# Three edits to the change-over between chunks: which queue stores the output projection's sums, where the last residual tile lies, and where the halo of h lies

## The chip, the cores and the metric

The kernel runs on one core of a Trainium2 chip. The metric is the device time of one execution in microseconds (us), as the median of several runs. Five engines work side by side, each through its own instructions in order: TensorE (PE; its weight loads are listed as PEld), VectorE (DVE), ScalarE (ACT), GpSimd (POOL) and SyncE (SP). SP does no arithmetic here; its queue issues most of the DMA transfers, and POOL's queue issues others between its arithmetic. An instruction that waits for a semaphore holds up everything behind it on its own engine's queue.

## The reference, cut to what matters

Two sequences go through a two-layer trunk: a prompt of 2048 rows and a sample of 512 rows, each row 1024 wide, in float32. Layer 0 is windowed attention, layer 1 a Fourier mixer, and a norm follows. The change lies wholly in layer 0:

```python
def attention_layer(x, g, w_in, w_out, sink, rel_bias):
    h = rmsnorm(x, g)
    z = h @ w_in                       # q (16 heads of 64), k, v (4 heads of 64), gate (1024)
    ...
    o = banded_gqa_with_sink(q, k, v, rel_bias, sink)   # |i-j| <= 128, blocks of 128
    return x + (o * silu(gate)) @ w_out
```

The last line is where the change sits: `x` there is the residual, the product with `w_out` is the output projection, and their sum is the input of layer 1.

## The kernel before, in words

**Chunks.** Layer 0 is done in five chunks of 512 rows, in the order of the list `CHUNKS`: chunk 0 is the sample, chunks 1 to 4 are the prompt. For the window, a chunk that has rows after it in its sequence (chunks 1, 2 and 3) also needs the keys and values of the next 128 rows, its halo. The change calls chunks 1, 2 and 3 the inner ones.

**Every matmul is three.** Operands are split into a high and a low float32r part (`matmul3`, L86 to L88), so each tile of h, q, of the probabilities, of u and of the weights is a pair.

**One chunk.** `make_h` (L171 to L183) loads eight tiles `xk` of the transposed input (512 rows and, with a halo, 128 more), POOL multiplies each by the inverse norms (L173), ACT and DVE make the two parts of `h` (L176, L177) and, where there is a halo, the two parts of `hl` (L182, L183). The `xk` tiles have four places (tag `x`), so the fifth load waits until the first `xk` has been read for both h and hl. `kv_proj` projects k (tiles `kp`, and `kh` for the halo) and v (`vp`); ACT and DVE evacuate k to `kwin` (L253, L254), `kh` (L275) and v (L300, L301). `qg_proj` makes q (`qab`, two places, L334 to L337) and the gate for one pair of heads at a time; eight pairs `p` follow one another. For each, scores (L388), exponentials (L400, L404), transposes of the probabilities into `pts` (tag `pt`, two places, L420 to L422), the product with v (`av`, L434), and the gated result in `uT` (tag `uT`, eight places, one for each pair, L442 to L452).

**The change-over.** `out_proj` multiplies the eight `uT` with `w_out`, in two halves of 512 columns. A half has eight steps `mm(half, k)`, which fill four PSUM banks `op`, and then `evac(half)` (L473 to L485): for each of four row tiles, the residual is loaded into an `xr` tile (L483), DVE adds the bank to it (L484) and the sum is stored to `x1d` (L485). `xr` has three places, so the fourth residual of a half waits for the store of the first. Chunks 0 to 3 issue these loads and stores on SP's queue. The last chunk issues them on POOL's, and there a list `res_tile` of two further tiles serves the fourth residual of each half. The first part of half 0 runs within the last pair's attention; the rest (the list `tail`) runs after the next chunk's `make_h` has been called, and before the next chunk's `kv_proj`. For the change-over from chunk 0 to 1 the tail is called before `make_h`.

**PSUM.** One pool of six banks (tag `bank`) serves `op`, `kp`, `kh`, `vp`, `pt`, `av` and the projections of q and the gate in turn. After half 1, `kp` takes two banks, `kh` one and `vp` up to four, so `vp` needs banks of half 1 whose sums have been made and the bank of `kh`.

**Weights.** From chunk 1 on, `load_w` (L94) loads each split weight tile of 1 MB in one DMA on SP's queue into one of four places (tag `w`). At the change-over these are `wo` for half 1, then `wk` and `wv`, two each, then `wq` and `wg`. `wk` holds four of the eight steps of the k projection in each tile.

**Order.** A planner orders the instructions of each engine beforehand, from the order in which the code calls them, from its own estimate of durations and from the places that come free. So what is called early may still be placed late on a queue, and what stands ahead on a queue can have been called later. `after(ins, anchor)` only tells the planner to place one instruction after another; it adds no wait.

**Layer 1** reads `x1d` from HBM after chunk 4; its first tiles are those of chunk 0.

Of the kernel before, what the change touches and what calls it, by code (L numbers as in the profile page):

```python
# [8 lines left out]
F32 = mybir.dt.float32  # L9
F32R = mybir.dt.float32r  # L10
# [3 lines left out]
ALU = mybir.AluOpType  # L14
# [4 lines left out]
P = 128  # L19
# [12 lines left out]
LINE = 512  # L32
# [3 lines left out]
CHUNKS = [(2048, SEQ, T), (0, 0, SEQ), (512, 0, SEQ), (1024, 0, SEQ), (1536, 0, SEQ)]  # L36


def f32(ap):
    return ap.bitcast(F32)  # L40
# [3 lines left out]
def encoder(  # L44
# [3 lines left out]
    PE, ACT, DVE, POOL, SP = nc.tensor, nc.scalar, nc.vector, nc.gpsimd, nc.sync  # L48
# [4 lines left out]
    wp = wstack.enter_context(tc.tile_pool(name="wp", bufs=1, side="right"))  # L53
# [12 lines left out]
    x1d = dram.tile([T, D], F32, name="x1d")  # L66
# [8 lines left out]
    def bank(name):  # L75
        return psum.tile([P, 512], F32, tag="bank", name=name)
# [7 lines left out]
    def matmul3(out, a, b, start, stop, more=False):  # L84

        PE.matmul(out, a[0], b[0], start=start, stop=False, skip_group_check=more)  # L86
        PE.matmul(out, a[0], b[1], start=False, stop=False, skip_group_check=more)  # L87
        PE.matmul(out, a[1], b[0], start=False, stop=stop, skip_group_check=more)  # L88

    def load_w(c, n, name, lo_engine=None, late=None):  # L90

        w = wp.tile([P, 2, D], F32R, align_bytes=LINE, tag="w", bufs=4, name=f"w{name}")
        if c:
            SP.dma_start(f32(w), f32(wsd[n]))  # L94
            return w[:, 0], w[:, 1]
        w32 = stage[late is not None or n > 19 or n in (6, 7, 18, 19)](f"w32{name}")
        load = SP.dma_start(w32, w_in[n] if n < 20 else w_out[(n - 20) // 4, (n - 20) % 4])
        if late:
            after(load, late)
        ACT.copy(w[:, 0], w32)  # L100
        if lo_engine is None:

            for i in range(4):
                cs = slice(i * 256, i * 256 + 256)
                POOL.tensor_tensor(w[:, 1, cs], w32[:, cs], f32(w[:, 0, cs]), ALU.subtract)
        else:
            lo_engine.tensor_tensor(w[:, 1], w32, f32(w[:, 0]), ALU.subtract)
        if late or n not in LATE:
            (SP if lo_engine else POOL).dma_start(f32(wsd[n]), f32(w))
        return w[:, 0], w[:, 1]  # L110

    stage, res_tile = [], []

    def after(ins, anchor):

        if anchor is not None:
            tc.add_manual_dep(ins.ins, anchor.ins.name, ISSUE, reason="issue order")

    def attention_phase():

        with ExitStack() as es:
            ap = es.enter_context(tc.tile_pool(name="attn", bufs=1))
# [19 lines left out]
            def spread(c, inv):  # L142

                tok, lo_t, hi_t = CHUNKS[c]
                nt = min(640, hi_t - tok) // P
                invb = ap.tile([P, 640], F32, tag="invb", name=f"invb{c}")
                for i0 in range(0, nt, 4):
                    m = min(4, nt - i0)
                    ps = bank(f"ib{c}_{i0}")
                    dg = ap.tile([P, 4, P], F32, tag="tmp", bufs=2, name=f"dg{c}_{i0}")  # L150
                    DVE.tensor_tensor(
                        dg[:, :m], ident.unsqueeze(1).to_broadcast([P, m, P]),
                        inv[:, i0 : i0 + m].unsqueeze(2).to_broadcast([P, m, P]), ALU.mult,
                    )
                    PE.matmul(ps[:, : m * P], ones, dg[:, :m].rearrange("p i q -> p (i q)"), start=True, stop=True)
                    ACT.copy(invb[:, i0 * P : (i0 + m) * P], ps[:, : m * P])
                return invb

            def make_h(c, invb):

                tok, lo_t, hi_t = CHUNKS[c]
                n = min(640, hi_t - tok)
                hs, halo = [], []
                for k in range(KD):
                    if invb is None:
                        if k % 2 == 0:
                            xk2 = wp.tile([P, 2, CH], F32, align_bytes=LINE, tag="uT", bufs=8, name=f"xk{c}_{k}")
                        xk = xk2[:, k % 2]
                    else:
                        xk = ap.tile([P, D], F32, tag="x", bufs=4, name=f"xk{c}_{k}")[:, :640]  # L170
                    SP.dma_start(xk[:, :n], xT[k * P : (k + 1) * P, tok : tok + n])  # L171
                    if invb is not None:
                        after(POOL.tensor_tensor(xk[:, :n], xk[:, :n], invb[:, :n], ALU.mult), last_evac[0])  # L173
                    h = main.tile([P, 2, CH], F32R, align_bytes=LINE, tag="hT", bufs=8, name=f"h{c}_{k}")
                    gk = g0s[:, k : k + 1]
                    ACT.activation(h[:, 0, :], xk[:, :CH], AF.Copy, scale=gk)  # L176
                    DVE.scalar_tensor_tensor(h[:, 1, :], xk[:, :CH], gk, f32(h[:, 0, :]), ALU.mult, ALU.subtract)  # L177
                    hs.append((h[:, 0], h[:, 1]))
                    if n > CH:
                        if k % 4 == 0:  # L180
                            hl = wp.tile([P, 4, 2, P], F32R, align_bytes=LINE, tag="uT", bufs=8, name=f"hl{c}_{k}")
                        ACT.activation(hl[:, k % 4, 0], xk[:, CH:], AF.Copy, scale=gk)  # L182
                        DVE.scalar_tensor_tensor(  # L183
                            hl[:, k % 4, 1], xk[:, CH:], gk, f32(hl[:, k % 4, 0]), ALU.mult, ALU.subtract
                        )
                        halo.append((hl[:, k % 4, 0], hl[:, k % 4, 1]))
                return hs, halo
# [7 lines left out]

            early = [load_w(0, 8, "k0_0", DVE)]
            hs, halo = make_h(0, None)
            early.append(load_w(0, 9, "k0_1", DVE))

# [25 lines left out]
            kwin = [kall[:, g] for g in range(4)]  # L225
            vblk = {}
            nS = [0]
            last_exp, last_evac = [None], [None]

            def scaled(ps, invb, name):  # L230

# [224 lines left out]
            def out_proj(c, uTs):  # L456
                tok = CHUNKS[c][0]
                steps = []
                st = {}

                def mm(half, k):
                    if k == 0:
                        st["ps"] = [bank(f"op{c}_{half}_{i}") for i in range(4)]
                    if k % 2 == 0:
                        st["w"] = load_w(c, 20 + half * 4 + k // 2, f"o{c}_{half}_{k}")
                    hi, lo = st["w"]
                    ws = slice((k % 2) * 512, (k % 2) * 512 + 512)
                    for i in range(4):
                        cs = slice(i * P, (i + 1) * P)
                        a = (uTs[k][0][:, cs], uTs[k][1][:, cs])  # L470
                        matmul3(st["ps"][i], a, (hi[:, ws], lo[:, ws]), k == 0, k == KD - 1)

                def evac(half):  # L473
                    for i in range(4):
                        rows = slice(tok + i * P, tok + (i + 1) * P)
                        cols = slice(half * 512, half * 512 + 512)
                        if res_tile and i == 3:
                            xt = res_tile.pop(0)
                        else:
                            xt = main.tile([P, 512], F32, tag="xr", bufs=3, name=f"xr{c}_{half}_{i}")  # L480

                        queue = POOL if c == len(CHUNKS) - 1 else SP
                        queue.dma_start(xt, x[rows, cols])  # L483
                        DVE.tensor_tensor(xt, xt, st["ps"][i], ALU.add)  # L484
                        queue.dma_start(x1d[rows, cols], xt)  # L485

                for half in range(2):
                    for k in range(KD):
                        steps.append(lambda half=half, k=k: mm(half, k))
                    steps.append(lambda half=half: evac(half))  # L490
                return steps
# [49 lines left out]
            for c in range(len(CHUNKS)):  # L541

                if c > 1:
                    hs, halo = make_h(c, invb)
                for s in tail:
                    s()
                if c == 1:
                    hs, halo = make_h(c, invb)
# [12 lines left out]
                for i in range(64 + LAG + AVLAG):  # L561
                    p, n = divmod(i, 8)
# [14 lines left out]
                    if c + 1 < len(CHUNKS):  # L577
# [4 lines left out]
                        elif i == 56:  # L582
                            invb = spread(c + 1, inv)
# [6 lines left out]
                    k = i - LAG  # L590
# [20 lines left out]
    def fourier_phase(tail):  # L611
        with ExitStack() as es:
# [502 lines left out]
            for i, f in enumerate(pend):  # L1115
                finish(*f, last=i == len(pend) - 1)

    fourier_phase(attention_phase())


# [96 lines left out]
```

## Time and profile before

The median of three runs is 1725.06 us (1722.04, 1725.06, 1725.29). The trace is of one more execution:

| what | value |
|---|---|
| time of the profiled execution | 1724.35 us |
| its span, first to last instruction | 1722.5 us |
| around the span | 1.85 us |
| mean granted TensorE clock | 0.986 |
| PE busy | 1661.5 us, 96% of the span |
| DVE, ACT, POOL busy | 1195.1, 862.8, 383.0 us |
| output sums (L484) | 40 adds, 0.68 us each |
| SP's stores of them, issue and landing | 32, 0.32 us each, 4.4 us to landing (median) |
| POOL's stores of `xr`, issue and landing | 6, 0.55 us each, 6.4 us to landing (median) |

A row of the waits view reads: who waited (engine, tile, line), then for whom, then the total, the number of waits and the longest, in us. A row of the timeline reads: start, duration, engine, line, operation, output and input, and how many were merged; a bracket gives the idle time before it and what ended it. A row of the windows view reads: the stretch, its length, the busy time of PE, PEld, DVE, ACT and POOL with instruction counts, the granted TensorE clock, the DMA share and GB/s.

### The profile page before, as it was taken

The numbers are of one execution on the slowest core, as the hardware profiler recorded it, in microseconds if no ns is written. First come the engines' busy times: TensorE is split into PE (matmuls) and PEld (weight loads), VectorE is DVE, ScalarE is ACT, GpSimd is POOL, SyncE is SP. The second block draws the span as 40 slices with busy tenths as digits, with TensorE's granted clock in tenths as the row PEclk, the third lists the DMA queues.
The fourth block names the chain that finished last, engine by engine and source line by source line (L and its number), as shares of the span: only waits on it lengthen the run. The fifth ranks groups of instructions, "written<-read, shape, count | busy, mean of one in ns | idle before, by whom it ended". The sixth has DMA issues, their size and how long they took to land. (4 is left out here: it accounts for less than half of the span.)

```text
span 1722.5 us, 25696 instructions
## 1 busy us (share of the span) xinstructions
PE 1661.5 (96%) x8980; PEld 1421.5 (83%) x8980; DVE 1195.1 (69%) x2814; ACT 862.8 (50%) x1966; POOL 383.0 (22%) x524
## 2 busy tenths in 40 slices
PE   9999899999989999899999999999999996999998
PEld 6877679888878888888888888877888885888886
DVE  5898655888538886378873688648676756888553
ACT  6677524666226664156751566536555534342221
POOL 2467641211303112121112211121111120111100
PEclk9999899999999999999999999999999998999999
DMA  8478776544575444763537734385556568563431
GB/s 308 164 285 316 266 284 217 183 176 162 190 261 183 176 171 148 279 230 129 187 141 277 264 135 146 116 334 194 185 199 229 190 231 327 175 226 120 141 107 49
DMA packets 94030, 348.88 MB, mean 203 GB/s; under 512 B 11292, under 2 KB 21532, under 8 KB 75981
## 3 DMA queue, kind: packets, MB, share of 16 engines
q1 hardware_dynamic: 77148, 275.14, 45.5%
q0 software_dynamic: 16176, 70.27, 10.5%
q10 hardware_dynamic: 576, 1.84, 0.4%
q8 instruction: 72, 1.18, 0.3%
q14 instruction: 58, 0.47, 0.1%
HBM read 269.57 MB, written 77.63 MB: 202 GB/s over the span
## 5 line engine op out<-in xcount | busy, mean ns | idle before, releaser
L404 ACT ACTIVATE S<-S 128x385 f32<-128x385 f32 (+1 forms) x320 | 191.2, 598 | 58.5 <-DVE S L400 57.6
L421 ACT CAST pts<-pt 128x384 fp32r<-128x384 f32 (+1 forms) x320 | 144.3, 453 | 113.2 <-PE pt L420 108.8
L422 DVE TENSOR_TENSOR pts<-pt,pts 128x384 fp32r<-128x384 f32 (+1 forms) x320 | 168.5, 527 | 43.4 <-ACT pts L421 40.6
L400 DVE CUSTOM_DVE_ANT_0 S<-spt,b 128x385 f32<-128x385 f32 (+1 forms) x320 | 168.8, 528 | 34.2 <-PE spt L388 29.7
L388 PE MATMUL spt<-kwin,qab 128*128 128x384 f32 (+1 forms) x640 | 158.8, 330 | 9.1 <-DVE S L400 9.1
L409 DVE TENSOR_SCALAR S<-S 128x384 f32<-128x384 f32 (+1 forms) x320 | 151.7, 474 | 9.1
L420 PE MATMUL pt<-ident,S 128*128 128x128 f32 x896 | 150.7, 274 | 0.6 <-DVE pts L422 0.4
L449 POOL TENSOR_TENSOR o<-o,s 128x256 f32<-128x256 f32 x75 | 55.3, 738 | 430.7 <-DVE o L445 424.4
L388 PEld LDWEIGHTS spt<-kwin,qab 128*128 128x128 f32 x640 | 118.4, 189 | 38.0 <-DVE S L400 12.8
L86 PE MATMUL gp<-h,wg 128*128 128x512 f32 x320 | 137.7, 430 | 0.0
L86 PE MATMUL qp<-h,wq 128*128 128x512 f32 x320 | 137.1, 428 | 0.6 <-ACT wq L100 0.6
L434 PEld LDWEIGHTS av<-pts,v 128*128 128x128 f32 x896 | 126.6, 189 | 11.5 <-DVE pts L422 0.2
L434 PE MATMUL av<-pts,v 128*128 128x256 f32 x896 | 135.2, 285 | 0.0
L86 PE MATMUL op<-wo,uT 128*128 128x512 f32 x320 | 126.9, 399 | 2.9 <-DVE xr L484 2.8
L420 PEld LDWEIGHTS pt<-ident,S 128*128 128x128 f32 x896 | 114.1, 141 | 16.3 <-DVE pts L422 4.3
L86 PE MATMUL fo<-wo,tTu 128*128 128x512 f32 x320 | 126.0, 394 | 1.3 <-ACT wo L634 1.2
L87 PE MATMUL op<-wo,uT 128*128 128x512 f32 x320 | 126.6, 396 | 0.0
L88 PE MATMUL qp<-h,wq 128*128 128x512 f32 x320 | 126.2, 394 | 0.1
L88 PE MATMUL op<-wo,uT 128*128 128x512 f32 x320 | 126.0, 395 | 0.0
L87 PE MATMUL fo<-wo,tTu 128*128 128x512 f32 x320 | 125.3, 392 | 0.7 <-DVE wo L635 0.6
L88 PE MATMUL gp<-h,wg 128*128 128x512 f32 x320 | 125.9, 394 | 0.0
L87 PE MATMUL qp<-h,wq 128*128 128x512 f32 x320 | 125.6, 393 | 0.0
(333 smaller groups left out, 4101.9 us busy)
## 6 DMA issues: line engine op xcount, KB each, us to landing
wq<-wsd SPq DMA_DIRECT2D x32, 1024.0 KB, 4.8
wg<-wsd SPq DMA_DIRECT2D x32, 1024.0 KB, 6.6
wo<-wsd SPq DMA_DIRECT2D x32, 1024.0 KB, 4.8
b<-b21d SPq DMA_DIRECT2D x40, 512.0 KB, 7.3
x<-x1d SPq DMA_DIRECT2D x38, 512.0 KB, 4.1
b<-rowd SPq DMA_DIRECT2D x40, 384.0 KB, 4.2
xs<-in_x_dram SPq DMA_DIRECT2D x23, 512.0 KB, 7.1
s2d<-gt POOLq DMA_DIRECT2D x40, 256.0 KB, 5.7
```

Of the source, the lines that this page charges most:

```text
L86: PE.matmul(out, a[0], b[0], start=start, stop=False, skip_group_check=more)
L87: PE.matmul(out, a[0], b[1], start=False, stop=False, skip_group_check=more)
L88: PE.matmul(out, a[1], b[0], start=False, stop=stop, skip_group_check=more)
L388: PE.matmul(ps[:, 2 + k0 * P : 2 + k1 * P], q, kwin[g][:, part, b * P + k0 * P : b * P + k1 * P], start=part == 0, stop=part == 1,)
L400: DVE.tensor_tensor_reduce(out=s[:, e0:e1], in0=ps[:, 1 + e0 : 1 + e1], in1=st["bias"][:, j, 386 - e1 : 386 - e0][:, ::-1], scale=1.0, sca ...
L404: last_exp[0] = ACT.activation(s[:, e0:e1], s[:, e0:e1], AF.Exp, bias=mn, scale=-1.0, accum_out=den)
L409: DVE.tensor_scalar(s[:, ks], s[:, ks], den, None, ALU.mult)
L420: PE.transpose(ps[:, kb, :], s[:, 1 + kb * P : 1 + (kb + 1) * P], ident)
L421: ACT.copy(hi[:, k0:k1, j, :], ps[:, k0:k1, :])
L422: DVE.tensor_tensor(lo[:, k0:k1, j, :], ps[:, k0:k1, :], f32(hi[:, k0:k1, j, :]), ALU.subtract)
L434: PE.matmul(out, v, pt[:, kb].rearrange("p h q -> p (h q)"), start=kb == k0 and part == 0, stop=kb == k1 - 1 and part == 1,)
L449: eng.tensor_tensor(of, of, res["s"][:, cs], ALU.mult)
```

## The change

Three things are altered, all in layer 0:

1. For the inner chunks the sums are stored by POOL's queue in place of SP's; the residual loads stay on SP's. The stores of half 1 are placed, on POOL's queue, after the last multiplication (L173) of the next chunk's `make_h`. Chunk 0 keeps SP for both, chunk 4 keeps POOL for both.
2. For the inner chunks the fourth residual of each half gets a tile of its own, two halves of one tile in a place of the probabilities (tag `pt`), by way of the list `res_tile` that only the last chunk used. So a half needs three `xr` tiles and not four.
3. The halo `hl` moves from the places of u (tag `uT`, eight places, in the pool `wp`) to the places of q (tag `qab`, two places, in the pool `ap`). Both tags have places of 4 KB per partition.

```diff
                     if invb is not None:
-                        after(POOL.tensor_tensor(xk[:, :n], xk[:, :n], invb[:, :n], ALU.mult), last_evac[0])
+                        last_mul[0] = POOL.tensor_tensor(xk[:, :n], xk[:, :n], invb[:, :n], ALU.mult)
+                        after(last_mul[0], last_evac[0])
...
                         if k % 4 == 0:
-                            hl = wp.tile([P, 4, 2, P], F32R, align_bytes=LINE, tag="uT", bufs=8, name=f"hl{c}_{k}")
+                            hl = ap.tile([P, 4, 2, P], F32R, align_bytes=LINE, tag="qab", bufs=2, name=f"hl{c}_{k}")
...
-            last_exp, last_evac = [None], [None]
+            last_exp, last_evac, last_mul = [None], [None], [None]
...
                 def evac(half):
+                    inner = 0 < c < len(CHUNKS) - 1
+                    if inner and half == 0:
+
+                        t = ap.tile([P, 2, 512], F32, align_bytes=LINE, tag="pt", bufs=2, name=f"xrl{c}")
+                        res_tile.extend((t[:, 0], t[:, 1]))
                     for i in range(4):
...
-                        queue = POOL if c == len(CHUNKS) - 1 else SP
-                        queue.dma_start(xt, x[rows, cols])
+                        (POOL if c == len(CHUNKS) - 1 else SP).dma_start(xt, x[rows, cols])
                         DVE.tensor_tensor(xt, xt, st["ps"][i], ALU.add)
-                        queue.dma_start(x1d[rows, cols], xt)
+                        store = (POOL if c else SP).dma_start(x1d[rows, cols], xt)
+                        if inner and half:
+                            after(store, last_mul[0])
```

## The prediction

> **What bounds the kernel now.** I read the shares of the engines first, then who waited on PE by stretches, then PE's own pace, and last the queues of SP and DVE at one change-over. On the page PE is busy almost throughout:
>
> ```profile
> PE 1661.5 (96%) x8980; PEld 1421.5 (83%) x8980; DVE 1195.1 (69%) x2814; ACT 862.8 (50%) x1966; POOL 383.0 (22%) x524
> ```
>
> So a saving counts only where PE stands or runs slowly. PE's waits from 440 to 540 us (chunk 1 to 2):
>
> ```profile
> PE vp L86 <- DVE xr L484: 2.1, 1, 2.1
> PE kp L86 <- DMA wk<-wsd: 2.0, 1, 2.0
> PE vp L86 <- ACT kh L275: 1.9, 1, 1.9
> ```
>
> From 670 to 775 us (chunk 2 to 3) the same three are 2.2, 0.6 and 1.9; chunk 3 to 4 has none, and chunk 0 to 1 has one other (2.8, PE op on DVE xr). The windows, from the first `kp` product to the first of q, for 1 to 2, 2 to 3 and 3 to 4:
>
> ```profile
> 470.00:501.60 31.60, 25.63 (x169) 24.80 (x169) 7.19 (x14) 4.89 (x12) 0.00 (x0) 0.89 0.81 288
> 703.20:733.70 30.50, 25.74 (x170) 24.91 (x169) 7.15 (x14) 4.87 (x12) 0.00 (x0) 0.89 0.83 295
> 934.60:951.60 17.00, 17.00 (x121) 16.96 (x121) 5.47 (x11) 4.27 (x10) 1.73 (x3) 1.00 0.96 358
> ```
>
> The clock, 1.00 in the third, is 0.89 in the first two: after the waits it is 0.50 from 488 to 492 us, and `vp` products there stand 0.21 us apart in place of 0.12. What is late shows in SP's timeline at 1 to 2:
>
> ```profile
> 468.09 0.32 SPq L485 DMA_DIRECT2D x1d<-xr  x1
> 468.51 2.26 SPq L483 DMA_DIRECT2D xr<-in_x_dram  x2
> 470.86 0.38 SPq L94 DMA_DIRECT2D wk<-wsd  x1
> 473.34 1.01 SPq L485 DMA_DIRECT2D x1d<-xr  x2
> 474.46 0.45 SPq L483 DMA_DIRECT2D xr<-in_x_dram  x1
> 475.00 0.74 SPq L94 DMA_DIRECT2D wv<-wsd  x1
> 481.00 0.32 SPq L485 DMA_DIRECT2D x1d<-xr  x1
> 481.41 0.38 SPq L483 DMA_DIRECT2D xr<-in_x_dram  x1
> 481.89 0.41 SPq L94 DMA_DIRECT2D wv<-wsd  x1
> ```
>
> and in DVE's:
>
> ```profile
> 472.63 1.38 DVE L484 TENSOR_TENSOR xr<-xr,op 128x512 f32<-128x512 f32 x2 [4.56 <-DMA xr<-in_x_dram]
> 480.29 0.69 DVE L484 TENSOR_TENSOR xr<-xr,op 128x512 f32<-128x512 f32 x1 [6.27 <-PE kp L88]
> 485.72 0.69 DVE L484 TENSOR_TENSOR xr<-xr,op 128x512 f32<-128x512 f32 x1 [4.74 <-DMA xr<-in_x_dram]
> 486.32 3.21 DVE L254 TENSOR_TENSOR kwin<-kp,kwin 64x384 fp32r<-64x384 f32 x6
> ```
>
> Each store on SP waits for its sum, and the next residual and the next weights stand behind it: from 450 to 500 us SP waits 22.4 us at L485. PE had ended half 1 at 470.06, yet its sums run to 486.4. (480.29 is put down to `kp`; the residual issued at 474.46 fits better.) `vp` waits for the banks, DVE's `kwin` stands behind the last sum, and ACT's copy of `kh` (488.95) behind `kwin`.
>
> **What these waits cost.** 48 `kp` products at 0.174 us, 24 `kh` at 0.120 and 96 `vp` at 0.120 make 22.75 us. The same prices give 16.99 us without a halo, where the trace has 16.97 (934.65 to 951.62). Chunk 1 to 2 took 31.61 us (470.06 to 501.67), 8.86 too long: 5.97 idle, the rest half clock. Chunk 2 to 3 took 30.42 (703.36 to 733.78), 7.67 too long: 4.76 idle. Together 16.5 us, and PE is the bound on both sides, so what goes here goes from the end.
>
> **Part 1, stores to POOL.** SP loses 24 issues of 0.32 us (7.7 us) and their waits; POOL gains 24 of 0.55 us (13 us of an engine 22% busy). On SP the weights follow as their places come free: half 1 takes 21.8 us, a `wo` tile lasts two steps (5.4 us), and the last `wo` was issued at 450.3. So the second `wk` can go at about 459 in place of 470.86, `wv` at 465 and 470 in place of 475.0 and 481.9. The second `wk` reached PE 5.5 us after issue; at 465 it is 9 us ahead of the fifth k step (474.2). That removes 2.0 and 0.6 us.
> Behind the stores of half 0 on POOL stand the multiplications of `xk` 4 to 7 (457.36 to 464.80). The sums of half 0 end by 452.2 but for the fourth, so POOL can be held some microseconds; h 7 was ready at 467.1 and is wanted at 477.3, 10 us of cover. The stores of half 1 stand behind multiplications that ended before their sums begin: nothing. Behind them POOL has nothing until 521.
> The store's landing sets when `xr` comes free: on POOL, in the last chunk, 5.3 to 11.6 us, median 6.5, against 5.5 on SP between 400 and 960 us. Issued at about 451 to 453 they land by 459, at worst 465. The loads of half 1 take 5.0 us (3.9 to 9.2): at PE by 464, at worst 474, wanted at 470. I take nothing. The Trainium skill (DMA: Bandwidth & Descriptors, SWDGE vs HWDGE vs iDMA) speaks against the move: GpSimd writes its descriptors to SBUF, which DVE locks it out of in two-port mode, and transfers from SP are immune. By it the stores would land later still; the 0.54 to 0.60 us of POOL's stores beside DVE's sums show no such hold.
>
> **Part 2, the fourth residual ahead.** It needs the place of the probabilities of the last pair's block 2, read by `av` until 441.8. SP stands at `wo` loads until 450.3, so it lands between 447 and 456. The sum, made at 467.39 before, moves to 452 to 456; the bank is wanted by `kp` at 470. All four residuals of half 1 are then there when PE ends, and the four sums take 2.7 us, to 472.8, before the `kwin` work at 478.4. That removes 2.1 and 2.2 us. The place is wanted again by `pts` at 518.9; the last store lands by 485: nothing.
> The `kh` wait: k ends at E; DVE's first `kwin` starts at E+0.5, and from it to the end of ACT's copy of `kh` passed 3.0 us, so E+3.5. The fourth `vp` block wants the bank after 24 `kh` and 9 `vp` products, E+3.96. Chunk 0 to 1, where `kwin` starts right after k, has no wait here. Bounds: nothing, by that row, to 1.90 idle and 2.9 at half clock at each of two. The margin of 0.46 is thin, so I take 0.5 each, 1.0 us.
>
> **Part 3, halo to q's places.** The same 24 ACT (0.39 us) and 24 DVE (0.35) instructions, but no wait for u: ACT sat 3.7 us for PE op before `hl`, at 452.81. The places are free (last scores of the pair 430.7, first halo 447) and wanted again at 507.6, after the halo's last product at 501.6: 6 us. `xk` 4 to 7 then load some 3 us sooner; h was not late, so nothing. The price is that `hl` may now stand on DVE ahead of the sums of half 0: between nothing and a delay of 6.6 us (four at the longest row, 1.66, which are those beside POOL's multiplications). POOL's first four end at 444.8, before `hl`, so I take the near end, nothing.
>
> **Sum.** 16.5 less 1.0 is 15.5 us. The profiled execution took 1724.35 (span 1722.5 and 1.85 around), 0.71 under the median; 1725.06 less 15.5 gives 1709.6.
>
> **Rivals.**
> *Half of it stays* (0.20). The residuals are in time, but ACT's copy of `kh` is not: 4.8 us stay at each, so 6.9 us are gained, 1718.2. The thin margin speaks for it, chunk 0 to 1 against.
> *No change* (0.08): the transfers are the limit, not the queue, and all land as late. The DMA share is 0.81 in the stretch, against it 0.08 from 464 to 468, when SP stood. Time 1725. The Trainium skill (DMA: Bandwidth & Descriptors, Issuing engines are not separate DMA queues) holds that all issuers share the same 16 DMA engines and that a second issuer saves only the sequencer's time. By that rule the 7.7 us of issue, beside PE, would be all; the 22.4 us of waits at L485 are what it leaves out.
> *Slower* (0.12): the planner puts `hl` ahead of the sums of half 0, at chunks 0 to 1, 1 to 2 and 2 to 3. Chunk 0 to 1 shows the price: there one DVE instruction took 3.38 us ahead of the second sum, and PE stood 2.85 us, then lost 1.7 at half clock (12 products in 4.46 us, not 2.73). Only 0.3 us of cover lay between (sum possible by 219.5, PE out at 219.8). A delay d costs 3 x (d - 0.3 + 1.7): at 6.6 us 24, so 7.5 us slower, 1732.6. It outweighs the gain from d = 4.1; four `hl` at their usual 0.31 in a row are 1.2.
>
> **Numbers.** My forecast has 0.60, with its own range 1705 to 1713 (below, if chunk 0 to 1's 4.6 us go too, as `xk` moves). With the first rival that is 0.80 faster. Within 0.2% (3.4 us, about what a measurement here can tell) 0.08, slower 0.12. The range 1705 to 1726 leaves out most of the slower case, the top of no change and a little below: some 0.18.
>
> **What would show it.** Right: both windows 22.8 us long at clock 1.00; no PE wait of `kp` on wk or `vp` on xr; half 1's `xr` loads on SP by 462 and its four sums in one row after PE's half 1; POOL stores near 0.55 us. Wrong: `hl` ahead of L484 on DVE with PE op waiting for xr, POOL's L173 held by a store, or a `kh` wait that stays.

## The result and the profile after

The changed kernel takes 1709.14 us (median of four runs, 1708.80 to 1711.04) where the kernel before takes 1725.17 (1722.04 to 1729.75): a ratio of 0.9907, 95% interval 0.9884 to 0.9931. The forecast was 1709.6 with a range of 1705 to 1726. The profiled execution of the changed kernel took 1711.04 us, the slowest of its four, with a span of 1709.0 and a mean granted clock of 0.99.

The shares of the engines on the page, after:

```profile
PE 1655.1 (97%) x8980; PEld 1416.9 (83%) x8980; DVE 1198.4 (70%) x2814; ACT 863.4 (51%) x1966; POOL 395.4 (23%) x548
```

PE has the same 8980 matmuls and is busy for 6.4 us less, about the 5.8 us that the prediction had put down to half clock; POOL has 24 instructions more, the stores. The windows from the first `kp` to the first q product, after, for the change-overs 1 to 2, 2 to 3 and 3 to 4 (columns as before: stretch, length, busy PE, PEld, DVE, ACT, POOL, clock, DMA share, GB/s):

```profile
470.30:494.70 24.40, 23.16 (x171) 22.83 (x170) 6.48 (x13) 5.11 (x12) 1.63 (x3) 1.00 0.89 341
695.90:718.70 22.80, 22.80 (x170) 22.80 (x169) 6.08 (x12) 5.07 (x12) 1.45 (x3) 1.00 0.92 350
919.70:936.70 17.00, 17.00 (x121) 16.96 (x121) 5.29 (x11) 4.29 (x10) 3.16 (x6) 1.00 1.00 407
```

The first two were 31.61 and 30.42 us long at clock 0.89 and are now 24.32 (470.35 to 494.67) and 22.81 (695.90 to 718.71) at 1.00; the third is as it was. That is 14.9 us. Of PE's waits in the first (440 to 540 us) one row is left, and in the second there is none:

```profile
PE kp L86 <- DMA wk<-wsd: 1.2, 1, 1.2
```

SP's timeline, after, at 1 to 2:

```profile
459.78 0.33 SPq L488 DMA_DIRECT2D xr<-in_x_dram  x1
...
460.68 8.50 SPq L488 DMA_DIRECT2D xr<-in_x_dram  x2
469.28 0.39 SPq L94 DMA_DIRECT2D wk<-wsd  x1
```

and DVE's:

```profile
453.92 5.60 DVE L178 SCALAR_TENSOR_TENSOR h<-xk,g0s,h 128x512 fp32r<-128x512 f32 x1 [1.10 <-ACT h L177]
...
459.70 0.68 DVE L489 TENSOR_TENSOR xr<-xr,op 128x512 f32<-128x512 f32 x1
460.30 0.67 DVE L489 TENSOR_TENSOR xrl<-xrl,op 128x512 f32<-128x512 f32 x1
...
473.09 0.68 DVE L489 TENSOR_TENSOR xrl<-xrl,op 128x512 f32<-128x512 f32 x1
480.39 3.85 DVE L255 TENSOR_TENSOR kwin<-kp,kwin 64x384 fp32r<-64x384 f32 x7 [6.62 <-ACT kwin L254]
```

The four sums of half 1 end at 473.8, and `kwin` starts 6.6 us later and waits for k alone, where before it stood behind the last sum (485.72). The fourth sum of half 0 is made at 460.30 (467.39 before). But the second `wk` goes out at 469.28, not at the forecast 459: one low part of h took 5.60 us on DVE beside POOL's multiplications, the third sum behind it came only at 459.70, and SP stood behind the residual of half 1 that takes this sum's place, until its store (issued at 460.67) had landed, 8.1 us later.

### The profile page after: what moved, and what is told of

Same layout as the page of the kernel before. It is cut to its first block, busy times and chain, and to the rows that moved or that the text cites. A ratio compares the mean times of both kernels' runs of the same rounds, so it can differ in the third digit from the quotient of the medians.

```text
span 1709.0 us, 25718 instructions
## 1 busy us (share of the span) xinstructions
PE 1655.1 (97%) x8980; PEld 1416.9 (83%) x8980; DVE 1198.4 (70%) x2814; ACT 863.4 (51%) x1966; POOL 395.4 (23%) x548
## 5 line engine op out<-in xcount | busy, mean ns | idle before, releaser
L86 PE MATMUL gp<-h,wg 128*128 128x512 f32 x320 | 137.7, 430 | 0.0
L86 PE MATMUL op<-wo,uT 128*128 128x512 f32 x320 | 127.3, 399 | 2.9 <-ACT uT L452 2.9
L87 PE MATMUL op<-wo,uT 128*128 128x512 f32 x320 | 126.1, 394 | 0.0
L88 PE MATMUL gp<-h,wg 128*128 128x512 f32 x320 | 126.0, 394 | 0.0
L87 PE MATMUL gp<-h,wg 128*128 128x512 f32 x320 | 125.5, 392 | 0.0
```

## The experiments

The question was which of the three parts brings the gain. Each was run alone, in pairs, and with pieces of it taken apart. In the table, "stretches" is the sum of the two windows at 1 to 2 and 2 to 3 in the profiled execution (the wait of the first `kp` for its weights added, where there is one; two times 22.75, 45.5, would be both undisturbed, at the prices of the prediction), and the ratio is to the kernel before on the same chip.

| kernel | stretches, us | median, us | ratio, 95% interval |
|---|---|---|---|
| before | 62.0 | 1722.5 to 1725.2 | 1 |
| part 1 | 57.6 | 1720.83 | 0.9993 (0.9981 to 1.0005) |
| part 2 | 47.9 | 1709.33 | 0.9926 (0.9907 to 0.9946) |
| part 3 | 47.8 | 1708.67 | 0.9917 (0.9900 to 0.9933) |
| parts 1 and 2 | 45.6 | 1711.15 | 0.9930 (0.9909 to 0.9951) |
| parts 1 and 3 | 61.5 | 1723.14 | 1.0002 (0.9988 to 1.0016) |
| parts 2 and 3 | 46.2 | 1709.21 | 0.9919 (0.9901 to 0.9937) |
| parts 2 and 3, again | 46.1 | 1708.38 | 0.9917 (0.9902 to 0.9932) |
| all three | 47.1 | 1709.14 | 0.9907 (0.9884 to 0.9931) |
| all three, again | 45.6 | 1710.16 | 0.9931 (0.9918 to 0.9944) |

### Part 1 alone

```diff
...
-                        queue.dma_start(x1d[rows, cols], xt)
+                        store = (POOL if c else SP).dma_start(x1d[rows, cols], xt)
+                        if inner and half:
+                            after(store, last_mul[0])
```

The lines that set `inner` and `last_mul` are those of the change.

> Part 1 alone: the inner chunks' sums are stored by POOL's queue; the fourth residual has no tile of its own and the halo stays in u's places. My theory, that each part removes the waits that the prediction gave to it: the waits of kp on wk go (2.0 and 0.6 us), those of vp on xr (2.1 and 2.2) and on kh (1.9 twice) stay, with most of the half clock, so 2.6 us less, about 1722. Rival A, that SP's queue alone was the cause and the weights and residuals follow freely once the stores have left it: all 16.5 us go, about 1709. Rival B, that a residual still waits for a store, which now lands later: no change or up to 3 us slower.

Measured: no clear difference, 0.9993. PE's waits at 1 to 2 in this kernel:

```profile
PE vp L86 <- ACT kh L276: 2.9, 1, 2.9
PE vp L86 <- DVE xr L485: 1.4, 1, 1.4
```

and the timelines of DVE and SP there:

```profile
467.34 0.68 DVE L485 TENSOR_TENSOR xr<-xr,op 128x512 f32<-128x512 f32 x1
...
468.86 1.27 DVE L485 TENSOR_TENSOR xr<-xr,op 128x512 f32<-128x512 f32 x2
...
482.81 0.69 DVE L485 TENSOR_TENSOR xr<-xr,op 128x512 f32<-128x512 f32 x1 [6.81 <-DMA xr<-in_x_dram]
483.42 3.83 DVE L255 TENSOR_TENSOR kwin<-kp,kwin 64x384 fp32r<-64x384 f32 x7
```

```profile
472.80 0.86 SPq L94 DMA_DIRECT2D wv<-wsd  x2
473.77 12.70 SPq L484 DMA_DIRECT2D xr<-in_x_dram  x4
```

SP is free, as foretold: both `wk` go out in one row from 458.67, and the wait for the second is gone. But the fourth sum of half 0 stands where it stood (467.34), and the third residual of half 1 waits for the landing of its store (out at 472.38). The fourth waits for the store of the half's own first sum. It goes out at 473.77, 7.6 us sooner than before, but right behind two `wv` of 1 MB, and lands only after some 9 us (4.2 before). So the last sum is made at 482.81, and `kwin` and the copy of `kh` stand behind it; that wait grew from 1.9 to 2.9 us. At 2 to 3 the order is the same: the residual goes out at 703.51 behind two `wv`, and its sum is made at 712.59. The stretches are 4.4 us shorter in this execution, and the medians 2.0. The interval reaches from 3.3 us less to 0.9 more, so it excludes the 16.5 us of rival A, and not the 2.6 us of the theory. The rule of the Trainium skill that the prediction weighed (DMA: Bandwidth & Descriptors, Issuing engines are not separate DMA queues), by which a second issuer saves only the sequencer's time, agrees with 0.9993 here; it leaves out that the second `wk` no longer stood behind a store that waited for its sum.

### Part 2 alone

```diff
...
+                    if inner and half == 0:
+                        t = ap.tile([P, 2, 512], F32, align_bytes=LINE, tag="pt", bufs=2, name=f"xrl{c}")
+                        res_tile.extend((t[:, 0], t[:, 1]))
```

> Part 2 alone: a tile of its own for the fourth residual of each half in the inner chunks; stores on SP, halo in u's places. My theory: the sums of half 1 follow PE at once, so SP's stores no longer hold anything for long; vp on xr and kh go with the half clock, kp on wk goes or stays under 2 us; 11 to 16 us less, 1709 to 1714. Rival A (the queue alone is the cause): the stores on SP still hold wk and the residuals, so less than 4 us, 1721 or more.

Measured: 0.9926, as much as the whole change. The fourth sum of half 0 is made at 451.94, the four sums of half 1 stand in one row from 468.10 to 470.8, and SP, which still has all the stores, sends both `wk` in one row from 463.20:

```profile
456.76 6.34 SPq L488 DMA_DIRECT2D xr<-in_x_dram  x3
463.20 0.86 SPq L94 DMA_DIRECT2D wk<-wsd  x2
```

What is left is one wait of `kp` for the first `wk`, 1.2 and 1.0 us. So the stores on SP were not themselves what held the weights; the late sum that one of them waited for was.

### Part 3 alone

```diff
-                            hl = wp.tile([P, 4, 2, P], F32R, align_bytes=LINE, tag="uT", bufs=8, name=f"hl{c}_{k}")
+                            hl = ap.tile([P, 4, 2, P], F32R, align_bytes=LINE, tag="qab", bufs=2, name=f"hl{c}_{k}")
```

> Part 3 alone: the halo in q's places; stores on SP, four residuals in three places. My theory: h and halo come some microseconds sooner, which nobody waits for; the three waits of PE stay, within 2 us of 1725. Rival C, that the late xk tiles, which hold the planner's fourth sum of half 0 behind h and halo on DVE, are the root: the fourth sum and all after it come sooner, 5 us less or more, 1720 or under. Rival D: the halo ahead of the sums of half 0 on DVE makes PE wait, slower by 2 to 7 us.

Measured: 0.9917, again as much as the whole, for the part that the prediction priced at nothing. DVE's timeline at 1 to 2:

```profile
459.96 0.34 DVE L184 SCALAR_TENSOR_TENSOR hl<-xk,g0s,hl 128x128 fp32r<-128x128 f32 x1
461.91 0.69 DVE L485 TENSOR_TENSOR xr<-xr,op 128x512 f32<-128x512 f32 x1 [1.61 <-DMA xr<-in_x_dram]
...
478.11 1.65 DVE L255 TENSOR_TENSOR kwin<-kp,kwin 64x384 fp32r<-64x384 f32 x3 [4.56 <-ACT kwin L254]
481.70 0.69 DVE L485 TENSOR_TENSOR xr<-xr,op 128x512 f32<-128x512 f32 x1 [1.94 <-DMA xr<-in_x_dram]
```

The fourth sum of half 0 is still the last of its row, behind all of h and the halo. But the halo no longer waits for a place of u, so `xk` 4 to 7 load at 447.83 (453.66 before), h 7 and its halo are done at 460.3 (467.5 before), and the sum follows at 461.91, held by its own residual now. SP's second `wk` goes out at 463.48. The last sum of half 1 is as late as ever (481.70), but three of `kwin` are placed ahead of it, so ACT's copy of `kh` comes at 481.00 (488.95 before), and only a wait of `vp` for `xr` stays: 0.8 and 1.0 us.

### Parts 2 and 3

> Parts 2 and 3 without part 1 (stores stay on SP). My theory: close to the whole change, the waits of vp on xr and kh gone, kp on wk at most 2.0 and 0.6 us: 1709 to 1713. Rival A (SP's queue is the cause): under 4 us less than before, 1721 or more. Rival E, that POOL's later landing costs what the leaving of SP gains: faster than the whole change by 1 to 3 us, 1706 to 1708.

Measured: 0.9919. The whole change without part 1 has both stretches at 22.81 and 22.85 us, with one wait of 0.6 us. The parts overlap: each alone brings nearly all that there is at this place.

### The whole change again

> The whole change once more, to stand beside the runs without part 1. If part 1 is worth anything where parts 2 and 3 are there, this is under 0.9919 of the time before by 2 us or more; my theory now is that it is worth nothing (it only moves a wait from vp to wk), so 0.990 to 0.993.

Measured: 1710.16, ratio 0.9931. Here both stretches are undisturbed (22.81 and 22.82 us), and the second `wk` goes out at 465.76, so the 1.2 us of the first profile is not in every execution. One low part of h took 5.60 us here as well; what differs is the landing of the third sum's store, 5.4 us here and 8.1 there.

### The fourth residual of one half only

Part 2's tile for half 0 only, and in a second kernel for half 1 only (`half == 1`):

```diff
+                    if 0 < c < len(CHUNKS) - 1 and half == 0:
+                        res_tile.append(ap.tile([P, 512], F32, align_bytes=LINE, tag="pt", bufs=2, name=f"xrl{c}"))
```

> The kernel before, and only the fourth residual of half 0 gets a tile of its own in the inner chunks; the fourth of half 1 still waits for an xr place. Theory now: the root is the fourth sum of half 0 (467.4 us before), which the planner sets behind h and halo on DVE, since its residual waits for a store; SP and the residuals of half 1 wait behind it. So this alone brings 10 us or more: the fourth sum of half 0 before 457, the three first residuals of half 1 in time, 1708 to 1715. Rival: the fourth residual of half 1 is what kwin and kh wait for, so under 5 us here.

> The kernel before, and only the fourth residual of half 1 gets a tile of its own in the inner chunks. Theory now: the fourth sum of half 0 stays at 467, the residuals of half 1 still come late and wk is still behind SP's store; the third sum at 480 rules in place of the fourth at 486; vp still waits, 3 to 7 us gained of 16. Rival: the last sum is all that matters, 12 us or more.

Measured: 0.9942 (0.9925 to 0.9960) and 0.9953 (0.9941 to 0.9965), stretches 48.5 and 50.4 us. With half 0 alone the sum of half 0 is made at 453.59 and what stays is the chain in half 1: its last sum comes at 481.14, and `vp` waits 1.4 us for the copy of `kh` behind it; at 2 to 3 the first `kp` waits 1.1 us for wk. With half 1 alone the sum of half 0 stays at 467.41, SP waits for it, the second `wk` goes out at 469.49, and `kp` waits 2.3 and 1.8 us for it. The two residuals have different waits. Yet either brings about two thirds of the gain, not half, since one wait that is left alone does not bring the half clock: the 25.31 us at 1 to 2 in the second kernel are 0.3 more than the products and the idle of 2.3 together.

### One DVE instruction moved

If both parts work by setting the fourth sum of half 0 free, then moving that sum ahead of h 4 to 7 on DVE, in the kernel before, should bring it without any new place:

```diff
+                    h_lo = DVE.scalar_tensor_tensor(h[:, 1, :], xk[:, :CH], gk, f32(h[:, 0, :]), ALU.mult, ALU.subtract)
+                    h_mid[:] = h_mid * (k > 4) + [h_lo] * (k >= 4)
...
+                        h_mid.extend([l_lo] * (k >= 4))
...
+                        add = DVE.tensor_tensor(xt, xt, st["ps"][i], ALU.add)
+                        [after(h, add) for h in h_mid if 0 < c < 3 and half == 0 and i == 3]
```

> The kernel before with one DVE instruction moved at the change-overs 1 to 2 and 2 to 3: the fourth sum of half 0 stands ahead of the low parts of h 4 to 7 and of their halo, in place of behind them. Nothing else is changed on any queue: stores on SP, four residuals in three places, halo in the places of u. Theory (parts 2 and 3 each work by setting this one sum free): its residual was issued at 456.49, so the sum is made at about 460 to 461 in place of 467.39, SP's store, the two residuals of half 1 and the second wk follow by 463 in place of 470.86, the waits of kp on wk and of vp on xr go, and the time is that of either part alone, 1708 to 1713, ratio 0.992 to 0.995. Rival (it is the extra place, or the earlier xk and h themselves): the two stretches stay above 28 us and the time within 3 us of the kernel before.

Measured: 1712.98, ratio 0.9937 (0.9918 to 0.9956). PE's waits at 1 to 2, and the rows of DVE and SP (in this execution the first `kp` is at 472.53, 2.5 us later than before, and SP's `wo` loads of this change-over, ahead of the moved sum, are as late already: 443.29 for 440.82):

```profile
PE vp L86 <- ACT kh L275: 2.1, 1, 2.1
```

```profile
465.63 0.69 DVE L483 TENSOR_TENSOR xr<-xr,op 128x512 f32<-128x512 f32 x1 [8.68 <-DMA xr<-in_x_dram]
466.23 0.74 DVE L177 SCALAR_TENSOR_TENSOR h<-xk,g0s,h 128x512 fp32r<-128x512 f32 x1
```

```profile
466.34 0.32 SPq L485 DMA_DIRECT2D x1d<-xr  x1
...
467.72 0.38 SPq L94 DMA_DIRECT2D wk<-wsd  x1
```

The sum now comes 6.9 us ahead of the first `kp`, where before it came 2.7 ahead: 4.2 us earlier, less than expected, because its residual took until 465.6 to arrive. That is enough: the waits for wk and for `xr` are gone at both change-overs, the clock is 1.00, and the stretches are 25.09 and 23.08 us. The copy of `kh` is late once, 2.1 us, since the chain in half 1 is untouched. So the place of one instruction of 0.68 us on DVE's queue accounts for most of the gain, and h, whose last low part now ends at 469.75, was indeed early enough, as the prediction had said.

### Parts 1 and 2, parts 1 and 3

> Stores by POOL and the fourth residual in its own tile, halo left in the places of u. Theory (the gains overlap, and part 1 moves a cost from SP to POOL): as part 2 alone, 1708 to 1711, ratio 0.992 to 0.994. Rival (part 1 adds, as the prediction had it): 2 to 3 us below part 2 alone, ratio 0.9905 to 0.9915, with no wait of kp on wk.

> Stores by POOL and the halo in the places of q, with four residuals of a half in three places. Theory (POOL's stores of half 0 stand among the multiplications and come after the halo on DVE): worse than part 3 alone, since the fourth residual now waits for a store on POOL, which lands later (6.4 us against 4.4): 1711 to 1717, ratio 0.994 to 0.997, with a wait of vp on xr longer than the 0.8 and 1.0 of part 3 alone. Rival (part 1 costs nothing): as part 3 alone, ratio 0.990 to 0.993.

> The whole change without part 1, a second time, beside the other pairs of parts. All theories: 1708 to 1711, ratio 0.991 to 0.993, since it had 0.9919 before. It is the measure by which the two pairs above are read in this job.

Measured: 0.9930 for parts 1 and 2, with no wait in either stretch (22.80 and 22.81 us): part 1 does take away the 1.2 and 1.0 us of wk that part 2 leaves, but two microseconds are below what the medians can tell. Parts 2 and 3 gave 0.9917 again.

Parts 1 and 3 gave 1.0002: part 1 undoes part 3 altogether, more than either theory expected. PE's waits at 1 to 2 are back:

```profile
PE vp L86 <- DVE xr L485: 3.2, 1, 3.2
PE vp L86 <- ACT kh L276: 2.9, 1, 2.9
```

POOL's timeline shows where it starts:

```profile
452.00 1.58 POOL L173 TENSOR_TENSOR xk<-xk,invb 128x640 f32<-128x640 f32 x1 [6.68 <-DVE hl L184]
453.52 0.64 POOL L486 DMA_DIRECT2D x1d<-xr  x1
```

The first sum of half 0, made at 451.88, is stored only after a multiplication. The list of DMA issues from 453 to 454.1 us has that store's landing, 8.7 us:

```profile
x1d<-xr POOLq DMA_DIRECT2D x1, 256.0 KB, 8.7
```

and in part 3 alone, from 451.3 to 452.5 us, SP's first two, 4.8:

```profile
x1d<-xr SPq DMA_DIRECT2D x2, 256.0 KB, 4.8
```

So the fourth residual, which waits for this place, goes out at 462.29, where part 3 alone has 457.24, and its sum is made at 465.01 for 461.91. Its own store lands after 7.5 us (4.0 in part 3 alone), and until then SP holds the third residual of half 1 (473.51 for 466.65) with both `wv` behind it. The last residual goes out at 475.09, sooner than the 476.41 of part 3 alone, but now right behind the two `wv`, and its sum is made 10.1 us later, where part 3 alone has 5.3. So the last sum comes 14.5 us after the first `kp` (485.23), where part 3 alone has 12.1; this time all of `kwin` stands behind it. In the whole change the fourth residual has its own place. The place of the first sum goes to the first residual of half 1, which is in time behind a landing of 6.7 us, and the same stores cost nothing that can be measured. The later landing was not general: six others of this change-over landed in 2.3 to 7.5 us.

### The multiplication at chunk 0 to 1

The change-over 0 to 1 keeps its wait of 2.9 us in the changed kernel; DVE's product `o` takes 3.38 us there, beside POOL's multiplications. To parts 2 and 3 was added:

```diff
-                    eng = DVE if p == 7 and b == 3 else POOL
+                    eng = DVE if p == 7 and b == 3 and c else POOL
```

> Parts 2 and 3, and in chunk 0 the last block's product with the gate and its low part go to POOL in place of DVE (two instructions moved), so that they stand on POOL's queue beside the multiplications of xk and not against them. Before, this DVE instruction took 3.38 us there, against 0.42 elsewhere, and PE stood 2.85 us and lost 1.7 more at half clock. Theory: DVE was held by POOL's multiplications; with POOL doing both in order the wait shrinks to 1 us or less and the clock stays: 3 to 4.5 us faster than parts 2 and 3, near 1705. Rival: POOL sets the product behind its multiplications (4.6 us for three), and PE waits as long or longer: 0 to 3 us slower.

Measured: 0.9928 (0.9912 to 0.9944), no better than without it. PE waits 0.6 and 2.5 us in place of 2.9. The low part of u, which follows on the same engine (L453), now stands on POOL behind two multiplications:

```profile
220.41 3.03 POOL L173 TENSOR_TENSOR xk<-xk,invb 128x640 f32<-128x640 f32 x2
223.41 0.72 POOL L453 TENSOR_TENSOR uT<-o,uT 128x256 fp32r<-128x256 f32 x1
```

The wait has changed its queue, not its length.

## Why the prediction was right, and where it was not

**The sum was right, and its closeness is partly luck.** 15.5 us were forecast; the medians moved by 16.0, and the two stretches by 14.9 in one profiled execution. In the repeat the stretches are 16.4 us shorter and the medians moved by 12.3, so half a microsecond is finer than these runs can tell. The stretches came to 24.32 and 22.81 where 22.8 each had been named, and the granted clock is 1.00 in both. That the waits cost more than their idle time is confirmed: 10.7 us of idle and 5.8 of half clock were in the price, and all but 1.2 us of the idle is gone.

**The kh step came out right, by 0.1 us.** It took 0.5 us at each change-over; there was no such wait in either profile of the whole change, and the stretch of 2 to 3 is 0.06 us above the products' prices. But the margin was not 0.46 us. With E as the start of the first `kh` product (480.21), the copy ends at E+3.84 (484.05) and not at E+3.5, and the first product that needs its bank starts at E+3.94 (484.15). That leaves 0.1 us, here and at the other change-over, in both profiles of the whole change.

**The halo ahead of the sums cost PE no wait of its own, but the delay was not small.** `hl` did go ahead of them on DVE, and the first sum moved from 450.28 to 451.54, 1.3 us. The third, behind h 4 and its halo as well, moved from about 451.5 to 459.70, 8.2 us, more than the 6.6 that the prediction had as its worst. `kp` wants the banks only at 470.35, so PE did not wait for the sum itself; SP waited for the landing of its store, and the 1.2 us of wk in the first profile came by that way.

**Part 3 was the step that failed.** "`xk` 4 to 7 then load some 3 us sooner; h was not late, so nothing." h was indeed not late for PE. But the fourth sum of half 0 stands behind h on DVE, SP's store waits for this sum, and the residuals of half 1 and the second `wk` stand behind the store. Whoever stands behind h on its queue was not asked. Alone this part brings the whole gain (0.9917), with `xk` sooner by 5.8 us where 3 had been written.

**Part 1's share does not show.** It was given 2.6 us for wk and credited with freeing SP. Alone it does remove the wait for wk, and the time moves by less than the runs can tell (0.9993, with 2.6 us still inside the interval); taken out of the whole it is not missed (0.9917 and 0.9919 without, 0.9907 and 0.9931 with). The 22.4 us that SP waits at its stores were not a cost of SP's queue: they were the lateness of the sums, seen from SP. The prediction added its parts as if each removed its own waits. Parts 2 and 3 both free the fourth sum of half 0, which is worth most of the gain by itself (0.9937), and part 1 moves what stands behind it. Part 2 also frees the last residual of half 1, and this alone, with that sum as late as ever, is worth 0.9953.

**Two sizes were off.** The second `wk` was forecast at 459 and went out at 469.28 and 465.76, so the cover of 9 us at the fifth k step was not there, and 1.2 us of wait stayed in one of the two profiles. The fourth sum of half 0, forecast at 452 to 456, came at 460.30. And "I take nothing" for the landing of POOL's stores held only because of part 2: in parts 1 and 3 a chain that begins with a landing of 8.7 us took all the gain away.

**The rivals.** Half of it staying is close to what part 1 alone did to `kh` (its wait grew to 2.9 us), not to the whole. The slower one, sums held behind the halo on DVE, needed a delay of 4.1 us at three change-overs with 0.3 us of cover. The third sum's delay was 8.2 at 1 to 2, but there the cover was 10 us. No change, the transfers as the limit, has something for it in part 1 alone, where SP was free and the last residual took some 9 us to land behind two `wv`; no run moved these loads alone.

What stays open: whether the two fates of `kwin` (three of them ahead of the last sum in part 3 alone, none in parts 1 and 3) come from the planner's order or merely cost what the order makes of a late residual; no run held the one fixed and changed the other.

## What to carry to other kernels

When several waits cluster at one change-over, look for an instruction that many of them stand behind, on whichever queue it is, and ask what stands ahead of it; here the queue that waited 22.4 us was only where the lateness was seen. Parts that ease the same late instruction overlap: price them one by one against each other, not as a sum, and run each alone, since here one DVE instruction set elsewhere is worth most of three edits. Where several short waits together lower the clock, taking away any one of them can bring more than its share. Before a store moves to another queue, ask who waits for the place that it frees: here the same move cost nothing measurable beside part 2, and took the whole gain of part 3.

## What was not expected of the hardware

**DVE beside POOL.** The low part of h takes 0.74 us alone and up to 2.1 beside POOL's multiplications in a row. In the three profiles where POOL's stores stand between these multiplications (parts 1 and 3, and both of the whole change), one h took 3.49, 5.59, 5.60, 5.62, 5.60 and 5.57 us, one at each of the change-overs 1 to 2 and 2 to 3; in the other profiles none took over 2.11 there. At 3 to 4 the stores stand between the multiplications in part 1 alone and in parts 1 and 2 too: one h took 4.75 and 4.78 us there, 4.79 in the whole change and 2.92 in parts 1 and 3, but none over 1.69 in the repeat of the whole change, with the same order on POOL. So it is frequent and not certain. At 0 to 1 one took 4.12 us where the product `o` stood on POOL among the multiplications, so it need not be a store. In the whole change it ends at 459.52, with the last multiplication ending at 458.96, so it was held through three of them. The Trainium skill (SBUF — State Buffer, SBUF: two separate sides) says that a DVE instruction with two SBUF inputs and a GpSimd one that reads SBUF exclude each other for a whole instruction; the 5.60 us agree with being shut out, but that rule does not say why h comes in after one multiplication in the one order and after three in the other, and no run settles it.

**The clock.** A single idle of PE of 2.1 us (the moved sum) or 2.3 us (half 1 alone) left the granted clock at 1.00 in its stretch. A single one of 2.85 us, at 0 to 1 in the kernel before, did not: the clock is 0.50 there from 224 to 226 us, and the products after it lost 1.7 us. Several shorter ones close together did not leave it at 1.00 either: idles of 0.6, 2.2 and 1.9 us within one stretch (before, 2 to 3) made it 2.9 us longer than products and idle together. Idles of 2.9 and 0.5 us (part 1 alone, 2 to 3) cost 2.0 beyond the idle itself, and 2.9 and 1.7 (parts 1 and 3, 2 to 3) cost 2.9. So here the first of several waits to go could be worth more than its idle time, and a last one of about 2 us no more than that. No run varies the length of a single idle between 2.3 and 2.85 us.
